# A weight sum queued behind an addition, and two norms' root products queued behind gate products, in the FFN inputs of a hybrid decoder layer

## The chip, the cores and the metric

The kernel runs on one core of a Trainium2 chip. The metric is device microseconds of one execution; three runs of the kernel before took 2287.8 to 2289.66 us, with a median of 2289.38 us. Lower is better. The engines are called as the profile calls them: PE is TensorE (PEld its weight loads), DVE is VectorE, ACT is ScalarE, POOL is GpSimd, and SP is SyncE, whose queue issues nearly all transfers.

## The reference

One layer for 1024 tokens of width 1024, all in float32: a SwiGLU half-step (ffn1), a mixer of three branches, and a second SwiGLU half-step (ffn2). Every part is normed before and after:

```python
def rms_norm(x, g):
    y = x * lax.rsqrt(jnp.mean(x * x, axis=-1, keepdims=True) + NORM_EPS)
    return y * g

def swiglu(u, w_in, w_out):
    gate, up = jnp.split(u @ w_in, 2, axis=-1)      # w_in: 1024 x 5632
    return (jax.nn.silu(gate) * up) @ w_out         # w_out: 2816 x 1024

f1 = swiglu(rms_norm(h, ffn1_pre_g), ffn1_w_in, ffn1_w_out)
h = h + 0.5 * rms_norm(f1, ffn1_post_g)
u = rms_norm(h, mix_pre_g)
# ... RWKV-7 time mixing, sliding-window attention and attention to memory,
#     all from u @ w_in, merged by gates and projected by w_out
h = h + rms_norm(merged @ w_out, mix_post_g)
f2 = swiglu(rms_norm(h, ffn2_pre_g), ffn2_w_in, ffn2_w_out)
h = h + 0.5 * rms_norm(f2, ffn2_post_g)
```

## The kernel before

**Products.** Activations lie with the features on the 128 partitions and the tokens on the free side, in two halves of 512 tokens (`TH`). A float32 product is made of three rounded ones: each operand is split into a high part (a cast on ACT, L277 for weights, L454 for activations) and a low part (a subtraction on DVE, L279 and L455), and `mm3` (L345) adds high x high, high x low and low x high into one PSUM bank (L348, L349, L350). A product of a weight operand (128 outputs, 4 blocks of 128 features) with a half of the activations is thus 4 x 3 = 12 matmuls.

**The seven products.** The FFN's products are done as 2 x 2 blocks with seven instead of eight block products. The activations' quarters are combined into factors (`b11`, `b21`, `t2`, `t1`, `t3`, `b22`, `t4`; made in `factors_first`, `factors_part` and `factors_end`, each then split), the weights' strips likewise. Only `b11` and `b21` need the first half of the tokens alone; all others need both halves, and so the second half's norm.

**The order of an FFN's input, `ffn_in` (L566).** First stand the norm of the second half (`norm`) and the factors. In ffn2 the norm is two: the mixer's post-norm and residual addition (`post_norm`), then the pre-norm (`factors_norm`). Then come the first two products of the gate for the first `FIRST` feature blocks j (9 in ffn1, 13 in ffn2), two products for each j, one with `b11` and one with `b21`: 18 and 26 products, 216 and 312 matmuls, which need no second half. Their results (`first`, L586) are copied out of PSUM by ACT and stored in DRAM (L587). After them come 22 steps (`ffn_in_pair`, L655). A step whose gate is already begun (kind "rest") makes five products in this order: t2 into px, t1 into pz, t3 onto px, b22 onto pz, t4 onto px. DVE copies px out with an addition after t2 (u, L673), pz after t1 (m, called z in the code), and adds px and z after t3:

```python
self.product(px, self.take(name, j), fs["t3"])
up = pool.tile([P, TH], F32, tag="up", name="up", bufs=2)
with self.tc.high_priority(offset=self.lead):
    V.tensor_tensor(up, px, z, ALU.add)                       # L686
self.product(pz, self.take(name, j), fs["b22"], last=True)
```

Then it adds pz (L689), multiplies by `up` (L691) and finishes the other half after t4. t4 writes onto px, so it waits for L686. The other steps (kind "pair") make their gate products themselves.

**The weights.** `operands` (L282) is a generator that loads raw strips (`raw`, five buffers, `w_raw`, loads on SP's queue, L268) and splits them; `take` lets it run eight operands ahead of the product (`OPS` = 8, buffers `w_hi`, `w_lo`). A step of kind "rest" needs four raw tiles a1, a2, b1, b2 and makes five operands of them: the first is the weight sum s = b1 + b2 (L303), then b1 = a1 - b1 (L304), a1 = s - a1 (L305), and a2 = a2 - a1 (L309). Since the generator runs eight operands ahead and a step uses five, the sum of step j + 2 is written in step j, just after `up`.

**The norms.** `inverse_root` (L426) takes the sum of squares, splits it (sq_hi on ACT, L438; sq_lo on DVE, L439), takes the mean over the partitions with two matmuls against a constant (the root products, L441), and forms the root with a logarithm, an exponential and a square on ACT (L444 to L446) and two DVE operations (L447, L448). It is used by all norms but the first over the memory and the last.

**What sets the order.** The program is written in one order; a planner then issues each engine's instructions in order of priority among those that are ready by its own reckoning of times, and puts in the semaphores. The priority is the place in the written order; `high_priority` moves what is written in it forward by some places (`lead` 300 for weights and parts of the chain, `urgent` 1000). `issue_after` keeps what it encloses behind a given instruction on that instruction's engine; `keep_in_program_order` keeps an instruction behind the one written before it on its engine. On the chip each engine works off its queue in the planned order and waits where an input is late.

Of the kernel before, what the change touches and what calls it, by code (L numbers as in the profile page):

```python
# [10 lines left out]
F32 = mybir.dt.float32  # L11
F32R = mybir.dt.float32r
I32 = mybir.dt.int32
ALU = mybir.AluOpType
# [15 lines left out]
SUMS = ("s1", "s2", "s3", "s4")  # L30
LAST_FORM = len(OUT_FORMS) - 1
FIRST = {"ffn1": 9, "ffn2": 13}
MIX_FIRST = (12, 13, 8, 4)
FILL = (18, 19, 14, 15)
HALVES = ((0, 0, TH), (1, 0, TH))
# [177 lines left out]
class Builder:  # L213
# [68 lines left out]
    def operands(self):  # L282
        V = self.nc.vector
        odd = False
        for name, i in self.seq:
            kind = name.partition("_")[2]
            odd = not odd and kind == "gate"
            a1 = self.raw(RAWS - 1 - (kind == "gate" and not odd))
            if kind == "out":
                kept = name == "ffn2_out" and i[0] == LAST_FORM and i[1] < KEEP  # L290
                yield (name, i), self.operand(a1, self.keep if kept else None)
                continue
            if kind == "gate":
                yield (name, i), self.operand(a1)
                continue
            a2 = self.raw(RAWS - 2)
            if kind != "rest":
                yield (name, i), self.operand(a1)
                yield (name, i), self.operand(a2)
            if kind in ("rest", "pair"):  # L300
                b1, b2 = self.raw(RAWS - 3), self.raw(RAWS - 4)
                s = self.sums.tile([P, 4, P], F32, tag="w_sum", name="w_sum", bufs=1)
                V.tensor_tensor(s, b1, b2, ALU.add)  # L303
                V.tensor_tensor(b1, a1, b1, ALU.subtract)  # L304
                V.tensor_tensor(a1, s, a1, ALU.subtract)  # L305
                yield (name, i), self.operand(a1)
                yield (name, i), self.operand(s)
                yield (name, i), self.operand(b1)
                V.tensor_tensor(a2, a2, a1, ALU.subtract)  # L309
                yield (name, i), self.operand(a2)  # L310
                yield (name, i), self.operand(b2)

    def prefetch(self, n=OPS, lead=None):
        with self.tc.high_priority(offset=self.lead if lead is None else lead):
# [30 lines left out]
    def mm3(self, out, w, x, first, last, **kw):  # L345
        (wh, wl), (xh, xl) = w, x
        mm = self.nc.tensor.matmul
        mm(out, wh, xh, start=first, stop=False, **kw)  # L348
        mm(out, wh, xl, start=False, stop=False, **kw)  # L349
        mm(out, wl, xh, start=False, stop=last, **kw)  # L350

    def project(self, w, u, outs, within={}):

# [72 lines left out]
    def inverse_root(self, sq, pool, between=None):  # L426
# [7 lines left out]
        with self.tc.high_priority(offset=self.lead):  # L434
            if not self.log_table:
                keep(S.preload_act_table_set("natural_log_exp_and_others"))
                self.log_table = True
            keep(S.activation(hi, sq, ACT.Identity, bias=self.eps))  # L438
            V.scalar_tensor_tensor(lo, sq, self.eps, hi.bitcast(F32), ALU.add, ALU.subtract)  # L439
            for i, x in enumerate((hi, lo)):  # L440
                mm = nc.tensor.matmul(ps, self.mean_r, x, start=i == 0, stop=i == 1)  # L441
                if between:
                    keep(mm)
            keep(S.activation(y, ps, ACT.Ln))  # L444
            keep(S.activation(y, y, ACT.Exp, scale=-0.5))
            keep(S.activation(sq, y, ACT.Square))  # L446
            V.scalar_tensor_tensor(sq, ps, -0.5, sq, ALU.mult, ALU.mult)  # L447
            V.scalar_tensor_tensor(y, sq, 1.5, y, ALU.add, ALU.mult)  # L448
# [117 lines left out]
    def ffn_in(self, f, x, form_d, first_d, parts, norm):  # L566

        nc, V = self.nc, self.nc.vector
        with self.tc.tile_pool(reuse_waits="tile", name="ffn_in", bufs=2) as pool:
            self.sums = pool  # L570
            self.factors_begin(pool)
            fs = self.fs
            for part in parts:
                norm(part, pool)
                self.factors_part(x, part, pool)
            self.factors_end(x)

            sums = {}
            for j, part in self.gate_order(FIRST[f]):
                if not part:  # L580
                    sums[j] = self.psum("px")
                self.product(sums[j], self.take(f + "_gate", (j, part)), fs["b21" if part else "b11"], not part, part > 0)
                tag, bufs = ("gate", 6) if part else ("px", 3)
                t = pool.tile([P, TH], F32, tag=tag, name="first", bufs=bufs)
                with self.tc.high_priority(offset=self.urgent):
                    nc.scalar.copy(t, sums[j])  # L586
                nc.sync.dma_start(first_d[j, part], t)  # L587
            self.log_table = False
            pairs = []
            for j in range(KF):  # L590
                *pair, made = self.ffn_in_pair(f, j, pool, first_d)
# [2 lines left out]
                    self.sums_made(f, j - FIRST[f], self.sums_loads(f, j - FIRST[f], pool, 4), made)  # L594
                if j % 2:
                    self.out_forms(j // 2, *pairs[-2:], pool, form_d)

    def sums_loads(self, f, q, pool, bufs):

# [55 lines left out]
    def ffn_in_pair(self, f, j, pool, first_d):  # L655
# [27 lines left out]
        self.product(px, self.take(name, j), fs["t3"])  # L683
        up = pool.tile([P, TH], F32, tag="up", name="up", bufs=2)
        with self.tc.high_priority(offset=self.lead):
            V.tensor_tensor(up, px, z, ALU.add)  # L686
        self.product(pz, self.take(name, j), fs["b22"], last=True)
        g1 = pool.tile([P, TH], F32, tag="gate", name="g", bufs=6)
        V.tensor_tensor(g1, pz, x, ALU.add)  # L689
# [954 lines left out]
    def build(self):  # L1644
        nc, tc, io = self.nc, self.tc, self.io
        with contextlib.ExitStack() as outer, tc.tile_pool(reuse_waits="tile", name="consts", bufs=1) as cp, \
# [2 lines left out]
            self.sum_d = {f: tc.dram_tile([len(SUMS), KP, P, KH, P], F32, name=f + "_sum_d") for f in ("ffn1", "ffn2")}  # L1649
            self.plan()  # L1650
            self.log_table, self.units, self.between = False, None, None
            self.vecs = cp.tile([P, NVEC], F32, name="vecs")
            nc.scalar.dma_start(self.vecs, io["vecs"])
            self.ones = cp.tile([P, 1], F32, name="ones")
# [138 lines left out]
```

## Time and profile before

| | |
|---|---|
| median of three runs | 2289.38 us (2287.8 to 2289.66) |
| the profiled execution's own time | 2288.03 us |
| its span, first to last instruction | 2286.3 us |
| mean granted clock of PE | 0.996 |
| PE busy | 2248.4 us, 98% |
| DVE, ACT busy | 1650.4 us, 996.6 us |
| transfers | 417.66 MB, 183 GB/s |

The profile is of one execution. In a list of waits, the columns are the waiting engine and its line, what ended the wait, the total in us, the number of waits, and the longest. In a timeline, they are the start in us from the span's start, the duration, engine, line, operation, output and inputs with their shapes and the count, and in brackets the idle time before it with what ended it. In a table of stretches, they are the stretch, its length, and the busy time with the number of instructions of PE, PEld, DVE, ACT and POOL, then the granted clock, the transfers' share and GB/s; a table for one tile on one engine has that engine alone. The tile z of the code appears as `m`, `x` as `u` or `px`, `up` as `up`. The gate products are the matmuls of px before the first step: from 40.2 us in ffn1 and from 1636.0 us in ffn2.

### The profile page before, as it was taken

What the parts mean: (1) busy time and instruction counts of PE and PEld (TensorE: products, weight loads), DVE (VectorE), ACT (ScalarE), POOL (GpSimd) and SP (SyncE); (2) the same over time, 40 slices, a digit from 0 to 9 for tenths busy, and PEclk for the clock granted to TensorE, in tenths of its full rate; (3) what the DMA queues carried; (4) which work ended last, traced back from release to release, by engine and by line L of the source; (5) the groups of instructions that cost most, each with busy time, mean ns of one, the idle gap of its engine ahead of it and who ended that gap; (6) DMA issues with size and microseconds to landing.
All of it is one profiled execution on the core that took longest, in us unless ns stands there. A gap on an engine that the chain in (4) does not pass through costs nothing.

```text
span 2286.3 us, 33447 instructions
## 1 busy us (share of the span) xinstructions
PE 2248.4 (98%) x11868; PEld 1842.3 (81%) x11868; DVE 1650.4 (72%) x2692; ACT 996.6 (44%) x1875; POOL 92.4 (4%) x138
## 2 busy tenths in 40 slices
PE   8999999999999999999999999999999999999998
PEld 6878888888888778888878877788788788888887
DVE  6987767666698885995665577675898885656676
ACT  5523333454555653223444454325663233345452
POOL 0000000000000000001320000041000000000000
PEclk9999999999999999999999999999999999999999
DMA  8565566686654466325436678755465552348663
GB/s 280 163 202 166 199 218 208 217 277 204 190 169 152 116 148 185 109 95 193 149 116 189 201 236 288 248 172 162 160 213 184 185 175 92 116 153 249 212 196 121
DMA packets 280775, 417.66 MB, mean 183 GB/s; under 512 B 82304, under 2 KB 104320, under 8 KB 280352
## 3 DMA queue, kind: packets, MB, share of 16 engines
q1 hardware_dynamic: 272832, 400.26, 55.2%
q10 hardware_dynamic: 7776, 15.28, 2.0%
q8 instruction: 93, 1.52, 0.3%
q14 instruction: 74, 0.61, 0.1%
HBM read 284.89 MB, written 129.50 MB: 181 GB/s over the span
## 4 chain that ended last, share of the span: by engine, by line
PE 77%; DVE 11%; DMA 7%; ACT 2%; issue 2%; SPq 0%; POOL 0%; DVEq 0%; ACTq 0%
PE px L348 6%; PE px L350 6%; PE px L349 6%; PE po L349 6%; PE po L348 6%; PE po L350 6%; PE pgate L348 3%; PE pgate L350 3%; PE pgate L349 3%; PE pz L348 2%; PE pz L350 2%; PE pz L349 2%; DMA w_raw<-in_ffn_in 2%; DVE w_lo L279 2%; PE pq L350 1%
## 5 line engine op out<-in xcount | busy, mean ns | idle before, releaser
L277 ACT CAST w_hi<-w_raw 128x512 fp32r<-128x512 f32 x594 | 366.8, 619 | 690.1 <-PE px L349 156.5
L279 DVE TENSOR_TENSOR w_lo<-w_raw,w_hi 128x512 fp32r<-128x512 f32 x594 | 411.7, 695 | 205.2 <-ACT w_hi L277 181.1
L350 PE MATMUL po<-u,w_lo 128*128 128x512 f32 (+1 forms) x476 | 180.9, 380 | 0.0
L349 PE MATMUL po<-u,w_hi 128*128 128x512 f32 (+1 forms) x476 | 180.9, 380 | 0.0
L348 PE MATMUL po<-u,w_hi 128*128 128x512 f32 (+1 forms) x476 | 180.9, 380 | 0.0
L348 PE MATMUL pgate<-u,w_hi 128*128 128x512 f32 x384 | 154.8, 403 | 0.0
L350 PE MATMUL pgate<-u,w_lo 128*128 128x512 f32 x384 | 151.5, 395 | 0.0
L349 PE MATMUL pgate<-u,w_hi 128*128 128x512 f32 x384 | 149.8, 390 | 0.0
L348 PE MATMUL px<-f,w_hi 128*128 128x512 f32 x352 | 138.0, 392 | 3.6 <-DVE up L686 2.7
L348 PE MATMUL px<-u,w_hi 128*128 128x512 f32 x352 | 137.0, 389 | 0.8 <-DVE km L1380 0.8
L348 PE MATMUL pz<-u,w_hi 128*128 128x512 f32 x352 | 137.0, 389 | 0.5 <-DVE m L673 0.5
L349 PE MATMUL px<-f,w_hi 128*128 128x512 f32 x352 | 137.2, 390 | 0.2 <-DVE f L455 0.2
L350 PE MATMUL px<-f,w_lo 128*128 128x512 f32 x352 | 137.0, 389 | 0.0
L350 PE MATMUL px<-u,w_lo 128*128 128x512 f32 x352 | 137.0, 389 | 0.0
L350 PE MATMUL pz<-u,w_lo 128*128 128x512 f32 x352 | 136.9, 389 | 0.0
L349 PE MATMUL px<-u,w_hi 128*128 128x512 f32 x352 | 136.9, 389 | 0.0
L349 PE MATMUL pz<-u,w_hi 128*128 128x512 f32 x352 | 136.9, 389 | 0.0
L455 DVE TENSOR_TENSOR u<-hid,u 128x512 fp32r<-128x512 f32 x114 | 78.3, 691 | 48.2 <-ACT u L454 47.5
L349 PEld LDWEIGHTS po<-u,w_hi 128*128 128x128 f32 x476 | 89.5, 188 | 17.2
L348 PEld LDWEIGHTS po<-u,w_hi 128*128 128x128 f32 x476 | 89.5, 188 | 17.1
L350 PEld LDWEIGHTS po<-u,w_lo 128*128 128x128 f32 x476 | 89.5, 188 | 16.8
L454 ACT CAST u<-hid 128x512 fp32r<-128x512 f32 x114 | 70.7, 620 | 66.2 <-DMA hid<-form_d 57.2
(391 smaller groups left out, 5125.8 us busy)
## 6 DMA issues: line engine op xcount, KB each, us to landing
w_raw<-in_ffn_in SPq DMA_DIRECT2D x220, 256.0 KB
hid<-form_d SPq DMA_DIRECT2D x154, 256.0 KB
w_raw<-in_win SPq DMA_DIRECT2D x112, 256.0 KB
form_d<-g SPq DMA_DIRECT2D x88, 256.0 KB
ws<-in_ffn_out SPq DMA_DIRECT2D x88, 256.0 KB
ffn_sum_d<-ws SPq DMA_DIRECT2D x88, 256.0 KB
w_raw<-ffn_sum_d SPq DMA_DIRECT2D x88, 256.0 KB
form_d<-h SPq DMA_DIRECT2D x66, 256.0 KB
```

Of the source, the lines that this page charges most:

```text
L277: self.nc.scalar.copy(hi, x)
L279: self.split_last = self.nc.vector.tensor_tensor(lo, x, hi.bitcast(F32), ALU.subtract)
L348: mm(out, wh, xh, start=first, stop=False, **kw)
L349: mm(out, wh, xl, start=False, stop=False, **kw)
L350: mm(out, wl, xh, start=False, stop=last, **kw)
L454: self.nc.scalar.copy(hi, x)
L455: self.nc.vector.tensor_tensor(lo, x, hi.bitcast(F32), ALU.subtract)
```

## The change

Two things change.

First, for steps of kind "rest" the weight sum L303 is written inside an `issue_after` on the latest `up` addition, so that on DVE it stands behind it (`behind_up`). Where no `up` has been written yet in this FFN, nothing is asked.

Second, the gate products become a generator (`gates_begin`) that gives back the last matmul of each `mm3`. The two root products of a norm are written inside an `issue_after` on one of these: the matmul that `PINS` names by its count, 78 for ffn1's norm, 42 and 114 for ffn2's two. `pinned` first writes as many gate products as that takes; so these, with their weights' loads, casts and splits and their copies and stores, now stand in the written order between the norm's split and its root products, ahead of the rest of the norm. What is left of the gate products follows the factors as before. The block of high priority in `inverse_root` is cut in two for this, in all norms.

```diff
+PINS = {"ffn1": (78,), "ffn2": (42, 114)}
...
                 s = self.sums.tile([P, 4, P], F32, tag="w_sum", name="w_sum", bufs=1)
-                V.tensor_tensor(s, b1, b2, ALU.add)
+                with self.behind_up(kind):
+                    V.tensor_tensor(s, b1, b2, ALU.add)
                 V.tensor_tensor(b1, a1, b1, ALU.subtract)
...
+    def behind_up(self, kind):
+
+        return self.tc.issue_after(self.up.ins) if kind == "rest" and self.up else contextlib.nullcontext()
...
-        mm(out, wl, xh, start=False, stop=last, **kw)
+        return mm(out, wl, xh, start=False, stop=last, **kw)
...
             V.scalar_tensor_tensor(lo, sq, self.eps, hi.bitcast(F32), ALU.add, ALU.subtract)
-            for i, x in enumerate((hi, lo)):
-                mm = nc.tensor.matmul(ps, self.mean_r, x, start=i == 0, stop=i == 1)
-                if between:
-                    keep(mm)
+        pinned = self.pinned()
+        with self.tc.high_priority(offset=self.lead):
+            with pinned:
+                for i, x in enumerate((hi, lo)):
+                    mm = nc.tensor.matmul(ps, self.mean_r, x, start=i == 0, stop=i == 1)
+                    if between:
+                        keep(mm)
             keep(S.activation(y, ps, ACT.Ln))
...
             self.factors_begin(pool)
-            fs = self.fs
+            self.gates_first, self.pins, self.gone = self.gates_begin(f, pool, first_d), list(PINS[f]), 0
             for part in parts:
                 norm(part, pool)
                 self.factors_part(x, part, pool)
             self.factors_end(x)
 
-            sums = {}
-            for j, part in self.gate_order(FIRST[f]):
...
-            self.log_table = False
+            for _ in self.gates_first:
+                pass
+            self.log_table, self.up = False, None
...
+    def gates_begin(self, f, pool, first_d):
+
+        nc, fs, sums = self.nc, self.fs, {}
+        for j, part in self.gate_order(FIRST[f]):
+            if not part:
+                sums[j] = self.psum("px")
+            w, x = self.take(f + "_gate", (j, part)), fs["b21" if part else "b11"]
+            for k in range(KH):
+                yield self.mm3(sums[j], tuple(t[:, k] for t in w), x[k], not part and k == 0, part > 0 and k == KH - 1, skip_group_check=True)
+            tag, bufs = ("gate", 6) if part else ("px", 3)
+            t = pool.tile([P, TH], F32, tag=tag, name="first", bufs=bufs)
+            with self.tc.high_priority(offset=self.urgent):
+                nc.scalar.copy(t, sums[j])
+            nc.sync.dma_start(first_d[j, part], t)
+
+    def pinned(self):
+
+        if not self.pins:
+            return contextlib.nullcontext()
+        n = self.pins.pop(0)
+        while self.gone < n:
+            behind, self.gone = next(self.gates_first), self.gone + 3
+        return self.tc.issue_after(behind.ins)
...
-            V.tensor_tensor(up, px, z, ALU.add)
+            self.up = V.tensor_tensor(up, px, z, ALU.add)
```

More of the change, by code (lines that the diff above doesn't have):

```diff
@@ L576, in ffn_in @@
             self.factors_end(x)
-            sums = {}
-            for j, part in self.gate_order(FIRST[f]):
[L580 to L587, printed above, removed]
-            self.log_table = False
+            for _ in self.gates_first:
+                pass
+            self.log_table, self.up = False, None
             pairs = []
@@ L1651, in build @@
             self.log_table, self.units, self.between = False, None, None
+            self.pins, self.up = [], None
             self.vecs = cp.tile([P, NVEC], F32, name="vecs")
```

## The prediction

> **What bounds the kernel now.** I read the page first, then what TensorE (PE) waited for, then VectorE's (DVE) waits, and then the timeline at the places which those name.
>
> ```profile
> span 2286.3 us, 33447 instructions
> PE 2248.4 (98%) x11868; PEld 1842.3 (81%) x11868; DVE 1650.4 (72%) x2692; ACT 996.6 (44%) x1875; POOL 92.4 (4%) x138
> PE 77%; DVE 11%; DMA 7%; ACT 2%; issue 2%; SPq 0%; POOL 0%; DVEq 0%; ACTq 0%
> ```
>
> PE is busy in 98% of the span and carries most of the chain. The change adds and removes no arithmetic, so all it can win are holes in PE's stream: 2286.3 - 2248.4 = 37.9 us at the very most. The waits of PE say which holes it can reach (columns: us in total, times, longest).
>
> ```profile
> PE ps_rs L441 <- ACT sq_hi L438: 3.9, 6, 1.5
> PE px L348 <- DVE up L686: 2.7, 5, 0.7
> PE px L348 <- ACT w_hi L277: 0.7, 2, 0.4
> PE pz L348 <- DVE m L673: 0.5, 1, 0.5
> PE px L349 <- DVE f L455: 0.2, 1, 0.2
> ```
>
> The first row is the root products that stand in PE's queue before their operand is there; the second and third are the last product of a step (t4), which adds onto px and so must wait until `up` has read it. The last two are waits on the norms' factors and on z, and will matter below.
>
> **Part 1: the sum behind `up`.** VectorE's own waits show what is in front of `up`:
>
> ```profile
> DVE w_sum L303 <- DMA w_raw<-in_ffn_in: 35.2, 27, 2.6
> ```
>
> The first weight sum waits for loads 27 times. One such place, VectorE first and then PE:
>
> ```profile
> 153.76 0.68 DVE L279 TENSOR_TENSOR w_lo<-w_raw,w_hi 128x512 fp32r<-128x512 f32 x1
> 157.03 0.69 DVE L303 TENSOR_TENSOR w_sum<-w_raw 128x512 f32<-128x512 f32 x1 [2.58 <-DMA w_raw<-in_ffn_in]
> 157.75 0.69 DVE L304 TENSOR_TENSOR w_raw<-w_raw 128x512 f32<-128x512 f32 x1
> 158.36 0.68 DVE L686 TENSOR_TENSOR up<-px,m 128x512 f32<-128x512 f32 x1
> 158.96 0.68 DVE L305 TENSOR_TENSOR w_raw<-w_sum,w_raw 128x512 f32<-128x512 f32 x1
> 161.01 0.68 DVE L689 TENSOR_TENSOR g<-pz,u 128x512 f32<-128x512 f32 x1
> ```
>
> ```profile
> 155.41 0.39 PE L350 MATMUL px<-f,w_lo 128*128 128x512 f32 x1
> 158.13 0.39 PE L350 MATMUL pz<-u,w_lo 128*128 128x512 f32 x1
> 159.19 0.47 PE L348 MATMUL px<-f,w_hi 128*128 128x512 f32 x1 [0.67 <-DVE up L686]
> ```
>
> px is complete at 155.41 + 0.39 = 155.8, `up` could run then, but VectorE sits at the sum until the load lands at 157.0, does the sum and L304, and reaches `up` at 158.36. PE has 12 matmuls of pz to hide behind (155.41 to 158.13, 2.72 us, so 0.227 each) and then stops: 1.06 us between starts instead of 0.23. The loss is 0.83 us, more than the 0.67 printed, since a matmul is recorded as 0.39 long but the next starts after 0.23. So each wait of this kind costs its idle time plus 0.16.
>
> With the sum behind `up`, `up` runs at 155.8 and ends before 156.6, 1.8 us before PE needs it: this hole closes. The two rows of px waits hold seven such holes, 2.7 + 0.7 = 3.4 us of idle, 3.4 + 7 x 0.16 = 4.5 us lost. (I count the two put down to w_hi here: the waits for `up` are the ones at the head of t4, and weights are fetched eight products ahead.) Holes too short to show as idle come on top, such as this pair, 0.52 apart, 0.29 lost:
>
> ```profile
> 1748.10 0.39 PE L350 MATMUL pz<-u,w_lo 128*128 128x512 f32 x1
> 1748.62 0.47 PE L348 MATMUL px<-f,w_hi 128*128 128x512 f32 x1
> ```
>
> That makes **-4.8 us**. [...]
>
> What is queued behind the sum, and now behind `up` as well: L304, L305, L309, the splits of the step's operands. The sum goes back by one VectorE addition at most where the load is late (0.69 us by its row), and by more only where the load was there first. It serves the step after the next; `up` of step j stands ahead of the sum of step j + 2. Seven products of 2.72 us, 19 us, lie between this sum and the first product that reads it, so I cost the delay at nothing; without that cover the 7 + 11 sums concerned would cost 18 x 0.69 = 12 us. The later releases of the raw buffers delay later loads by as much, under the same cover. What is late next is the following step's u and z, behind whatever VectorE still owes; through the steps it is not full,
>
> ```profile
> 106.90:200.00 93.10, 91.27 (x398) 74.11 (x398) 76.85 (x124) 29.62 (x50) 0.00 (x0) 1.00 0.58 191
> ```
>
> 76.85 of 93.10 us (the third pair), so it works off what gathers behind a late load, two or three additions, within a step. Bounds of the part: 0 and -5.3 (two more short holes of about 0.25).
>
> **Part 2: the pins.** In ffn1, PE, then ScalarE (ACT), then VectorE:
>
> ```profile
> 55.48 0.39 PE L349 MATMUL px<-u,w_hi 128*128 128x512 f32 x1
> 57.37 0.50 PE L441 MATMUL ps_rs<-sq_hi,mean_r 128*128 128x512 f32 x1 [1.50 <-ACT sq_hi L438]
> ```
>
> ```profile
> 56.59 0.72 ACT L438 ACTIVATE sq_hi<-sq,eps 128x512 fp32r<-128x512 f32 x1 [0.44 <-DVE sq L468]
> 58.75 0.60 ACT L444 ACTIVATE rs<-ps_rs 128x512 f32<-128x512 f32 x1 [1.43 <-PE ps_rs L441]
> 60.24 0.62 ACT L277 CAST w_hi<-w_raw 128x512 fp32r<-128x512 f32 x1
> 60.75 0.64 ACT L446 ACTIVATE sq<-rs 128x512 f32<-128x512 f32 x1
> ```
>
> ```profile
> 60.89 0.69 DVE L279 TENSOR_TENSOR w_lo<-w_raw,w_hi 128x512 fp32r<-128x512 f32 x1 [2.79 <-ACT w_hi L277]
> ```
>
> The hole is 57.37 - 55.48 - 0.23 = 1.66 us. In ffn2 there are two:
>
> ```profile
> 1643.71 0.39 PE L349 MATMUL px<-r,w_hi 128*128 128x512 f32 x1
> 1644.76 0.50 PE L441 MATMUL ps_rs<-sq_hi,mean_r 128*128 128x512 f32 x1 [0.66 <-ACT sq_hi L438]
> ...
> 1668.93 0.39 PE L349 MATMUL px<-u,w_hi 128*128 128x512 f32 x1
> 1669.81 0.50 PE L441 MATMUL ps_rs<-sq_hi,mean_r 128*128 128x512 f32 x1 [0.49 <-ACT sq_hi L438]
> ```
>
> 0.82 and 0.65 us. How many gate matmuls stand ahead of each root product (stretches of px alone, count in brackets):
>
> ```profile
> 40.10:55.70 15.60, 15.51 (x68) 1.00 0.72 228
> 1636.00:1643.90 7.90, 7.89 (x35) 1.00 0.43 138
> 1644.90:1669.20 24.30, 24.03 (x105) 1.00 0.79 262
> ```
>
> Now 68, 35 and 35 + 105 = 140; the pins ask for 78, 42 and 114. Ten more in ffn1 are 2.27 us: the product starts near 55.48 + 11 x 0.227 = 57.98, after its operand (57.31). Seven more in ffn2: 1645.5 against 1644.8 now. Neither delays the second half of the root by more than 0.1. The third pin, 114, is already met by 140 and binds nothing; that hole closes only if the planner keeps its distance of 105 from the first root, now seven later. So up to 1.66 + 0.82 + 0.65 = 3.13 us of holes go.
>
> But what comes next is late too. After the roots VectorE has the factors to make and hardly a gap:
>
> ```profile
> 61.50:94.30 32.80, 32.80 (x146) 27.18 (x145) 32.71 (x55) 18.68 (x34) 0.00 (x0) 1.00 0.58 178
> 1674.00:1709.40 35.40, 35.40 (x158) 29.32 (x157) 35.27 (x59) 23.10 (x43) 0.00 (x0) 1.00 0.57 177
> ```
>
> The third pair of figures is VectorE's: 32.71 of 32.80 and 35.27 of 35.40 us. PE reaches the first products on those factors sooner, and where VectorE has not moved it waits there (the f and m rows above). In ffn1 VectorE does move: tracing the gates first puts the cast of 60.24 ahead of the logarithm, into ScalarE's 1.43 us idle, so the square of 60.75 comes about 0.5 earlier and the split of 60.89 falls into VectorE's 2.79 us of idle: about 0.5 + 0.6 = 1.1. I keep 1.0 of 1.66 (ends: 0 and 1.66). In ffn2 no such shift shows; I keep 0.6 of 1.47 (ends 0 and 1.47). Part 1 helps ffn1 once more: the sum stands between two factors,
>
> ```profile
> 98.98 0.68 DVE L455 TENSOR_TENSOR f<-t,f 128x512 fp32r<-128x512 f32 x1
> 99.69 0.69 DVE L303 TENSOR_TENSOR w_sum<-w_raw 128x512 f32<-128x512 f32 x1
> 100.31 0.68 DVE L455 TENSOR_TENSOR f<-t,f 128x512 fp32r<-128x512 f32 x1
> ```
>
> and steps out of their way (0.6 us of VectorE); I count it as part of the 1.0.
>
> Gate work now traced ahead of the rest of the norm: its loads and the copies' stores pass the residual's stores on SP's queue, its casts and copies the norm's operations on ScalarE, its splits those on VectorE. Casts and splits wait for operand buffers that PE frees one per product, so few can pass; I take 0, bounds -0.6 to +1.2 (one split earlier, two splits ahead of the factors). POOL gets nothing. The other norms have no pin; their root products only move by a few places in priority, taken as 0.
>
> **Sum.** -4.8 - 1.0 - 0.6 = -6.4 us against the profiled execution's 2288.03 (span 2286.3): 2281.6. The median of the runs lies 1.35 above it, so **2283.0**.
>
> **The rivals.**
> *The wait is handed on.* `up` is free, but VectorE still stands at the sum until the load lands, and L689, L691 and the next step's u and m queue behind it; PE stops there instead. [...] Against: L689 has until its px and pz buffers come round, and that z waits only once (0.5) today. It leaves the pins' 1.6: 2287.8.
> *The pins give everything back.* PE only arrives sooner at factors that are as late as before. For: the full stretches. Against: the idle 2.79. Part 1 alone: 2289.38 - 4.8 = 2284.6.
> *The change does not do what it says.* The planner had put the roots where the inputs are ready by its reckoning and moves other work with them; nothing is left: 2289.
> *Slower: the gate splits crowd the norm.* Traced first, they pass the factors on a VectorE that is full from 61.5 to 94.3. Each takes 0.6 (98.98 to 99.69 is one place); PE waits for the last factor. It decides from 6.4 / 0.6 = 11 splits that pass; at 20 the kernel is 5.6 us slower, 2295. Against: the buffers let one pass per product.
>
> **Chances and range.** Forecast 0.54, its own range 2280.8 to 2284.7; handed on 0.13; given back 0.14; nothing 0.08; slower 0.11. About 0.2%, 4.6 us, is what a measurement of this kernel can tell: faster means below 2284.8. That is the forecast and most of the given-back case: 0.64; within: 0.26; slower (0.11, less the cases of it that cost little): 0.10. The low end takes every hole: 4.8 + 0.5 + 3.13 + 0.6 = 9.0, so 2280.3; the high end reaches to the cases with no gain, 2289.5.
>
> **What would show it.** Right: no px wait for `up` in the waits of PE; `up` directly ahead of L303 in VectorE's order in steps with loads, and still about 35 us of waits for w_raw; the roots behind 78, 42 and about 147 gate matmuls with no idle ahead; px and pz waits for f and m grown by 1 to 2 us. Wrong: waits of PE for w_lo or u in the steps, factors later by more than PE gained, or a different order in the mixer.

## The result

The changed kernel takes 2280.31 us (median; 2272.83 to 2281.52) where the kernel before takes 2289.38 us beside it: a ratio of 0.9956, 95% interval 0.9944 to 0.9968. It is faster by 0.44%, some 10 us by the ratio and 9.07 by the two medians; the forecast was 2283.0, 6.4 us less than before. The direction was right, and so was which holes close; how much of them is kept was not: the median lies at the end of the range that stood for "every hole goes" (2280.3), and by the ratio (0.9956 x 2289.38 = 2279.3) the time lies 1 us below it.

The profiled execution took 2280.59 us. Its page, in the lines that answer to those shown of before:

```profile
span 2278.6 us, 33469 instructions
PE 2244.7 (99%) x11868; PEld 1843.1 (81%) x11868; DVE 1648.2 (72%) x2692; ACT 994.9 (44%) x1875; POOL 92.1 (4%) x138
PE 86%; DVE 7%; DMA 4%; ACT 2%; issue 2%; SPq 0%; POOL 0%; DVEq 0%; ACTq 0%
```

The instructions are the same 11868 matmuls and 2692 of VectorE. PE's share of the chain went from 77 to 86%, VectorE's from 11 to 7. What PE waited for (us in total, times, longest), and below it the wait of VectorE for the weights of the sum:

```profile
PE ps_rs L450 <- ACT sq_hi L444: 1.5, 4, 0.6
...
PE px L355 <- DVE f L464: 0.8, 1, 0.8
...
PE px L354 <- DVE up L711: 0.6, 1, 0.6
```

```profile
DVE w_sum L305 <- DMA w_raw<-in_ffn_in: 9.4, 14, 1.3
```

VectorE's wait for PE ahead of `up`, before and after:

```profile
DVE up L686 <- PE px L350: 38.0, 24, 1.7
```

```profile
DVE up L711 <- PE px L356: 52.5, 36, 1.7
```

The lines have moved: the sum L303 is now L305, `up` L686 is L711, the root product L441 is L450, sq_hi L438 is L444, u and m L673 are L698, the splits' L455 is L464. Of the px waits for `up` one of 0.6 us is left, in the last pair of ffn1 (457.90 us), outside the steps of kind "rest"; no root product of the FFN inputs waits any more (the four that are left are in other norms). The second fence holds what the prediction did not foresee: it expected about 35 us of waits for w_raw to stay, and 9.4 are left. The idle time has in part moved: VectorE waits 52.5 us ahead of `up` where it waited 38.0. The place that corresponds to the one the prediction showed, VectorE and then PE:

```profile
150.90 0.68 DVE L280 TENSOR_TENSOR w_lo<-w_raw,w_hi 128x512 fp32r<-128x512 f32 x1
152.73 0.69 DVE L711 TENSOR_TENSOR up<-px,m 128x512 f32<-128x512 f32 x1 [1.14 <-PE px L356]
153.51 0.69 DVE L305 TENSOR_TENSOR w_sum<-w_raw 128x512 f32<-128x512 f32 x1
```

```profile
155.02 0.39 PE L356 MATMUL pz<-u,w_lo 128*128 128x512 f32 x1
155.25 0.39 PE L354 MATMUL px<-f,w_hi 128*128 128x512 f32 x1
```

VectorE now idles for PE's product and no longer for the load, `up` starts as soon as px is complete, and by the time `up` is done the load is there, so the sum waits for next to nothing. PE goes from pz to t4 in 0.23 us. The three roots:

```profile
56.73 0.39 PE L356 MATMUL px<-r,w_lo 128*128 128x512 f32 x1
56.95 0.39 PE L450 MATMUL ps_rs<-sq_hi,mean_r 128*128 128x512 f32 x1
...
1642.81 0.39 PE L356 MATMUL px<-u,w_lo 128*128 128x512 f32 x1
1643.04 0.39 PE L450 MATMUL ps_rs<-sq_hi,mean_r 128*128 128x512 f32 x1
...
1668.20 0.39 PE L355 MATMUL px<-r,w_hi 128*128 128x512 f32 x1
1668.42 0.44 PE L450 MATMUL ps_rs<-sq_hi,mean_r 128*128 128x512 f32 x1
```

They stand behind 78, 42 and 152 gate matmuls, 0.22 to 0.23 us after the matmul before them. All three holes are shut.

Where the time went, stage by stage, in us from the start of a stage's first matmul to that of the next stage's. "Before 2" and "after 2" are later profiles of the same two kernels; the other columns are experiments told below. The last row is no part of the change: the mixer between the two FFNs.

| stage | before | before 2 | after | after 2 | sum alone | pins alone | no edge | ffn2's pins |
|---|---|---|---|---|---|---|---|---|
| ffn1 gates | 51.42 | 50.20 | 49.50 | 49.58 | 50.48 | 49.53 | 50.39 | 50.65 |
| ffn1 steps 0, 1 | 27.86 | 28.34 | 28.48 | 29.02 | 27.76 | 28.75 | 27.93 | 27.59 |
| ffn1 steps 2 to 8 | 98.30 | 97.15 | 95.20 | 95.20 | 95.20 | 98.19 | 95.20 | 95.20 |
| ffn2 gates | 73.48 | 73.46 | 71.79 | 71.85 | 73.48 | 71.86 | 73.48 | 71.86 |
| ffn2 step 0 | 14.36 | 14.18 | 13.79 | 13.94 | 14.19 | 14.42 | 13.60 | 13.78 |
| ffn2 steps 1 to 12 | 166.36 | 166.25 | 163.21 | 163.22 | 163.20 | 166.96 | 163.20 | 163.21 |
| sum of these | 431.78 | 429.58 | 421.97 | 422.81 | 424.31 | 429.71 | 423.80 | 422.29 |
| mixer | 869.23 | 868.68 | 871.11 | 867.84 | 866.54 | 868.62 | 868.04 | 863.25 |

The mean of the two profiles of before is 430.68, of the two of after 422.39: 8.3 us, 0.36%, which both measured intervals of this kernel (here and in the second group below) hold. The mixer differs by up to 8 us between runs, so a single pair of spans would not do. 95.20 and 163.2 us are floors at the steady pace of these steps, in which no 12 matmuls in a row, start to start, took less than 2.71 us in the first profiles of before and after: steps 2 to 8 are 7 x 60 = 420 matmuls and steps 1 to 12 are 720, and at 0.2267 us each (12 in 2.72 us, as in the prediction) these take 95.2 and 163.2.

### The profile page after: what moved, and what is told of

It is laid out like the page before. It is cut to its first block, busy times and chain, and to the rows that moved or that the text cites. A ratio compares the mean times of both kernels' runs of the same rounds, so it can differ in the third digit from the quotient of the medians.

```text
span 2278.6 us, 33469 instructions
## 1 busy us (share of the span) xinstructions
PE 2244.7 (99%) x11868; PEld 1843.1 (81%) x11868; DVE 1648.2 (72%) x2692; ACT 994.9 (44%) x1875; POOL 92.1 (4%) x138
## 4 chain that ended last, share of the span: by engine, by line
PE 86%; DVE 7%; DMA 4%; ACT 2%; issue 2%; SPq 0%; POOL 0%; DVEq 0%; ACTq 0%
PE px L354 7%; PE px L355 7%; PE px L356 7%; PE po L355 6%; PE po L354 6%; PE po L356 6%; PE pz L356 3%; PE pz L354 3%; PE pz L355 3%; PE pgate L354 3%; PE pgate L356 3%; PE pgate L355 3%; PE pq L355 1%; PE pq L356 1%; PE pq L354 1%
## 5 line engine op out<-in xcount | busy, mean ns | idle before, releaser
L464 DVE TENSOR_TENSOR u<-hid,u 128x512 fp32r<-128x512 f32 x114 | 78.3, 690 | 47.1 <-ACT u L463 46.1
```

Source lines behind the costliest of these rows:

```text
L464: self.nc.vector.tensor_tensor(lo, x, hi.bitcast(F32), ALU.subtract)
```

## The experiments

**The parts.** Four kernels ran on one chip with the kernel before, 2286.46 us there. The sum alone:

```diff
-PINS = {"ffn1": (78,), "ffn2": (42, 114)}
+PINS = {"ffn1": (), "ffn2": ()}
```

> Part 1 alone: the sums stand behind up, no root product is pinned and the gate products are written where they were. If the holes at t4 simply close (my present theory): the steps of kind rest get shorter by about 3.1 us in ffn1 and 3.1 us in ffn2, as in the changed kernel, the gate stretches keep their three holes (1.66, 0.82, 0.65), and the whole is 6.2 us faster. If the prediction's term was right: 4.8 us. If the wait is handed on: the steps keep their length, with PE waiting for m, u or w_lo, and the whole is within 1 us of before.

2277.83 us, ratio 0.9965 (0.9951 to 0.9978). Both stretches of steps are at their floors, 95.20 and 163.20; the gates keep their holes. So part 1 is worth 3.10 + 3.16 = 6.26 us against the first profile of before, and 1.95 + 3.05 = 5.0 us against the second, whose holes in ffn1 were fewer. The pins alone:

```diff
-        return self.tc.issue_after(self.up.ins) if kind == "rest" and self.up else contextlib.nullcontext()
+        return self.tc.issue_after(self.up.ins) if False else contextlib.nullcontext()
```

> Part 2 alone: the roots are pinned at 78, 42 and 114, the sums stay ahead of up. Present theory: the gate stretch gets 1.9 us shorter in ffn1 and 1.7 in ffn2; the first step gives 0.6 back in ffn1 and nothing in ffn2, the t4 holes stay, and the whole is 3 to 3.5 us faster. The prediction's term: 1.6 us, with 0.7 given back in ffn1 and 0.9 in ffn2. If the pins give everything back: 0.

2282.60 us, ratio 0.9985 (0.9975 to 0.9996). The steps stay at least as long as before (98.19 and 166.96); the gates lose what they lose in the changed kernel. The two parts act on different stages, and by the ratios they add: 0.35 + 0.15 = 0.50% against 0.44 (0.32 to 0.56). By the stretches, against the mean of the two profiles of before, the sum alone wins 6.4 us, the pins alone 1.0 and both 8.3: in the one profile of the pins alone, the steps lose 1.9 of the 2.9 us that the gates win.

**The edge without its effect on PE.** The gate products are written as early as in the changed kernel, but the root products are bound to none:

```diff
-        return self.tc.issue_after(behind.ins)
+        return contextlib.nullcontext()
```

> The changed kernel without the edges that hold the root products back; the gate products are still written ahead of them. If the edge is what closes the holes: the roots stand behind 68, 35 and 140 gate matmuls again, with holes of 1.66, 0.82 and 0.65 us, and the whole is like part 1 alone, about 6.2 us faster than before. If the written order is what brings it: no holes, about 9 us faster.

2278.35 us, ratio 0.9975 (0.9963 to 0.9986). The roots stand behind 68, 35 and 140 gate matmuls again, as before, and the gate stretches are 50.39 and 73.48. So the edge, not the place in the written order, moves the roots and shuts the holes. Step 0 of ffn2, however, has 13.60 us here and 13.78 to 13.94 with pins in ffn2, against 14.19 with the sum alone, one profile each: the wait for z there (0.5 us in the waits of before) goes because the gate products are written earlier, and needs no pin. (With the pins alone, step 0 has 14.42 us: the wait for z is gone there too, but PE waits for a factor instead: 0.9 us in two waits for f in that profile, 0.2 in one in before.)

**Later pins.**

```diff
-PINS = {"ffn1": (78,), "ffn2": (42, 114)}
+PINS = {"ffn1": (102,), "ffn2": (66, 114)}
```

> The changed kernel with the first root of each FFN pinned 24 gate matmuls later (102 and 66), 24 x 0.227 = 5.4 us. If the full VectorE behind the roots is the bound, as the prediction had it: what PE does behind the gate products is 5.4 us later in both FFNs, in all 10.9 us slower than the changed kernel. If the factors are finished well before their products in ffn2 (they were by 8 us in the kernel before): 3 to 5 us slower in ffn1 and under 1 us in ffn2.

2286.96 us, ratio 0.9999 (0.9985 to 1.0013): the gain is gone. But not where it was expected: the gate stretches are 49.54 and 71.80 us, as in the changed kernel, and the first steps cost 1 us more in ffn2 and nothing in ffn1 (14.75 and 28.47). The loss lies steps later, 99.26 us for steps 2 to 8 and 171.17 for 1 to 12. PE, VectorE and SP's queue at the largest place:

```profile
1748.45 0.39 PE L356 MATMUL pz<-u,w_lo 128*128 128x512 f32 x1
1753.72 0.80 PE L354 MATMUL px<-f,w_hi 128*128 128x512 f32 x1 [4.88 <-DVE u L698]
```

```profile
1745.96 0.69 DVE L662 TENSOR_TENSOR h<-g,h 128x512 f32<-128x512 f32 x1
1752.97 0.69 DVE L698 TENSOR_TENSOR u<-px,m 128x512 f32<-128x512 f32 x1 [6.32 <-DMA m<-first_d]
```

```profile
1746.68 0.32 SPq L664 DMA_DIRECT2D form_d<-h  x1
1747.05 0.45 SPq L664 DMA_DIRECT2D form_d<-g  x1
1747.55 1.24 SPq L689 DMA_DIRECT2D m<-first_d  x2
```

PE waits for u, u for the stored gate product m, and the reload of m was issued at 1747.55 only, behind stores (L664) of what VectorE had just finished at 1746.65. The edit has changed the order of SP's queue too: with these pins the third reload of m in ffn2 stands behind seven of those stores, in the changed kernel behind one.

**The changed kernel again, and four small changes of it,** on a second chip, where the kernel before took 2286.98 us. First the kernel itself:

> The changed kernel once more, on the chip on which the others of this group run, so that they are compared with it and not only with the kernel before. Theory A (the gain is a property of the two edits): 0.9955 to 0.9965 of the kernel before, with step stretches of 95.2 us in ffn1 and 163.2 us in ffn2 (98.3 and 166.4 before). Theory B (a good part of the measured gain was a faster clock in some runs): 0.998, with the same stretches but a longer mixer. Theory C (the pins are worth nothing beside the sum): the same 0.9965 as the sum alone had, to 0.0005.

2276.86 us, ratio 0.9962 (0.9947 to 0.9977), with the stretches of the table. Theory A holds; the mixer was 867.84, not longer than in before, so theory B has no support. Theory C can't be told from A by the times; by the stretches the pins bring 424.31 - 422.39 = 1.9 us.

The third pin left out:

```diff
-PINS = {"ffn1": (78,), "ffn2": (42, 114)}
+PINS = {"ffn1": (78,), "ffn2": (42,)}
```

> The third pin left out, so ffn2's second root product is bound to no gate product. The prediction's theory (the third pin is met anyway and binds nothing): the second root still stands behind 152 gate matmuls with no idle time ahead, ffn2's gate stretch stays at 71.8 us, and the time is that of the changed kernel within 0.5 us. Rival (the pin's tracing of gate work ahead of the second norm is what keeps the distance): the 0.65 us hole comes back, 72.4 us, and step 0 of ffn2 goes from 13.8 to 14.4 us.

2280.53 us, ratio 0.9969 (0.9957 to 0.9982); ffn2's gates take 71.84 us, step 0 14.05. The stretch between the two roots (its length, and PE's busy time with the count of px) is

```profile
1637.55:1662.60 25.05, 24.87 (x110) 1.00 0.84 280
```

110 matmuls, with the 42 before them 152, as with the pin. It binds nothing.

The sum behind `up` in steps of both kinds:

```diff
-        return self.tc.issue_after(self.up.ins) if kind == "rest" and self.up else contextlib.nullcontext()
+        return self.tc.issue_after(self.up.ins) if self.up else contextlib.nullcontext()
```

> The sum stands behind the addition of px and z in steps of both kinds. In the planned order this moves it in one place of each FFN. The wait-goes theory: the one wait for the addition that is left in the changed kernel, 0.96 us between starts near 457 us of ffn1, goes as the seven others did: 0.7 us less in the stretch of ffn1's pairs, nothing in ffn2, 2279.5 where the changed kernel has 2280.3. The handed-on theory: the next sums and splits are late, and PE waits for w_lo in the pair behind, 0 to +0.5 us.

2279.81 us, ratio 0.9972 (0.9963 to 0.9982). No wait for `up` is left, but none is in the second profile of the changed kernel either, and VectorE's work ahead of that `up` is a split (L464 at 456.56 us, after 1.17 us of idle for ScalarE), not a sum. So this run shows nothing of the edit; the expectation had taken a wait of one execution for a property of the kernel. It does show something of ffn1's pin: ScalarE waited 2.36 us for the store ahead of the squares (0.88 and 1.57 in the two profiles of the changed kernel), the root product, behind 78 gate matmuls as there, came 0.38 us after the matmul before it, and its second half waited again (0.79 us between starts). The gates took 50.36 us, as without the pin. So 78 shuts ffn1's hole only while that store is not later than it was in the other runs.

Four more VectorE instructions in the factors of each FFN (the output is unchanged, but the planner also moves other work), 2.4 us by an estimate of 0.6 each, the distance of three 128x512 subtractions on VectorE in the changed kernel (starts at 118.14, 118.74 and 119.34 us):

```diff
-            V.tensor_tensor(self.t2[k], x21[k], self.t2[k], ALU.subtract)
+            V.tensor_tensor(self.t2[k], x21[k], self.t2[k], ALU.subtract); V.tensor_tensor(self.t2[k], self.t2[k], self.t2[k], ALU.max)
```

> Four more VectorE instructions (the maximum of a tile with itself, 128x512, 0.6 us each) in the factors of each FFN: 2.4 us more for VectorE behind the roots, the output unchanged. Theory full engine (the prediction's: VectorE is full behind the roots, so PE must wait for whatever is later there): steps 0 and 1 of ffn1 go from 28.5 to 30.9 us and step 0 of ffn2 from 13.8 to 16.2 us, 4.8 us in all. Theory due times (VectorE works ahead of PE in ffn2; the last factor of t4 starts at 1717.8 us, 1.8 us before PE needs it): ffn1, where PE already waits 1.2 us for a factor, pays 1.8 to 2.4 us, and ffn2 pays 0 to 0.6 us.

2286.43 us, ratio 0.9993 (0.9981 to 1.0005). In ffn2, step 0 takes 14.27 us (13.78 to 14.05 in the kernels with the sum's edge and these pins) and steps 1 to 12 163.22: at most 0.5 of the 2.4 us, so a full VectorE is not what PE waits for there. In ffn1 steps 0 and 1 take 28.11, no more than in the changed kernel, and there both theories fail: the price, 7.05 us, is paid in steps 2 to 8 (102.25 us), by one hole. PE, VectorE, SP's queue, and PE's clock behind the hole (stretch, length, busy times with counts, granted clock):

```profile
127.34 0.39 PE L356 MATMUL pz<-u,w_lo 128*128 128x512 f32 x1
132.24 0.79 PE L354 MATMUL px<-f,w_hi 128*128 128x512 f32 x1 [4.51 <-DVE u L698]
```

```profile
125.94 0.69 DVE L662 TENSOR_TENSOR h<-g,h 128x512 f32<-128x512 f32 x1
131.49 0.69 DVE L698 TENSOR_TENSOR u<-px,m 128x512 f32<-128x512 f32 x1 [4.87 <-DMA m<-first_d]
```

```profile
124.72 2.25 SPq L664 DMA_DIRECT2D form_d<-h  x3
127.02 0.45 SPq L664 DMA_DIRECT2D form_d<-g  x1
127.52 1.25 SPq L689 DMA_DIRECT2D m<-first_d  x2
```

```profile
132.30:137.00 4.70, 4.70 (x11) 3.73 (x12) 1.08 (x2) 0.00 (x0) 0.00 (x0) 0.50 0.12 45
```

It is the picture of the late pins: 4.90 - 0.23 = 4.67 us of hole, and then 11 matmuls in 4.70 us where 4.70 / 0.2267 = 20.7 would run, another 9.7 x 0.2267 = 2.2 us.

The two pictures share one more thing, which the times alone hide. In the changed kernel the third reload of ffn1 went out ten microseconds sooner, behind a single store:

```profile
117.05 0.33 SPq L664 DMA_DIRECT2D form_d<-g  x1
117.42 0.43 SPq L689 DMA_DIRECT2D m<-first_d  x1
```

In the busier kernel it stands behind all seven stores of that pair of steps, the last of them at 127.02. The planner had put it there, so four added instructions changed the order of SP's queue and not only the times. In every kernel with its reloads on SP's queue that has no such hole, before and the changed kernel among them, the third reload of each FFN stands behind one store; with the late pins it stands behind two in ffn1 (a hole of 2.50 - 0.23 = 2.27 us) and behind seven in ffn2 (5.04 us). The busier kernel's ffn2, where the same four instructions cost 0.5 us at most, kept the old order.

**The reload on another queue,** to see whether SP's order makes the price. On a third chip, before at 2285.97 us there; in the busier kernel and in the one with the late pins:

```diff
-            nc.sync.dma_start(m1, first_d[j, 0])
-            nc.sync.dma_start(g0, first_d[j, 1])
+            nc.gpsimd.dma_start(m1, first_d[j, 0])
+            nc.gpsimd.dma_start(g0, first_d[j, 1])
```

> The busier kernel (four more VectorE instructions in the factors), with the reloads of the stored gate products (the tile m and its gate) issued from GpSimd's queue and not from SP's. In the busier kernel steps 2 to 8 of ffn1 took 102.25 us where the changed kernel has 95.20, with one wait of TensorE of 4.5 us for u; u waited for a reload that SP issued at 127.52 us, behind stores of products which VectorE finished at 126.6; the buffer of the reload was free from 124.1. Theory queue (2.4 us of VectorE became 7 because the reload stood behind those stores): the reload goes out 3.4 us earlier, the wait falls from 4.5 to about 1 us, the stretch to 96 to 98 us, the time to 2281 to 2283 on a chip where the busier one has 2286.4. Theory backlog (VectorE owes the work, the queue is nothing): the stretch stays at 101 to 103 us and the time at 2286.

2294.37 us, ratio 1.0042 (1.0027 to 1.0058).

> The kernel with the late pins (102 and 66), with the same reloads on GpSimd's queue. With the late pins steps 2 to 8 of ffn1 took 99.26 and steps 1 to 12 of ffn2 171.17 us (95.20 and 163.21 in the changed kernel). Theory queue (the late pins cost little by themselves; the cost is the reload behind the stores): most of 4.1 + 8.0 us goes, the stretches fall to 95.2 to 97 and 163.2 to 167 us, the time from 2287 to 2279 to 2282. Theory backlog: they stay within 1 us of what they were.

2298.18 us, ratio 1.0056 (1.0035 to 1.0078). Both are slower, against the queue theory; the backlog theory has one stretch right and neither time. In the busier kernel the hole itself shrank, from 4.67 to 1.58 us: the reload was issued at 121.52, as soon as its buffer was free, and not at 127.52, and landed 4.5 us later. (The 124.1 of the expectation is when the buffer of the next reload came free.) What PE waits for is still u:

```profile
124.98 0.39 PE L356 MATMUL pz<-u,w_lo 128*128 128x512 f32 x1
126.79 0.50 PE L354 MATMUL px<-f,w_hi 128*128 128x512 f32 x1 [1.42 <-DVE u L698]
```

but steps 2 to 8 took 102.21 us all the same and ffn2's steps 173.08 (163.22 without the move), by new waits. VectorE's wait for the sum's weights, in the kernel with the reloads moved and then in the busier kernel:

```profile
DVE w_sum L305 <- DMA w_raw<-in_ffn_in: 39.4, 24, 5.3
```

```profile
DVE w_sum L305 <- DMA w_raw<-in_ffn_in: 7.4, 15, 1.0
```

With the late pins the hole of 5.04 us in ffn2 became one of 3.26 - 0.23 = 3.03, that in ffn1 grew from 2.27 to 2.60 us, and the stretches 100.37 and 177.66. So the reload's place in SP's queue is a part of the hole's length in two of three places, but its price could not be taken away by this edit, since SP's order changed with it and weights came late instead. What makes those loads late was not tried, nor was a kernel in which the third reload alone is put back behind the first store, so what the planner's order costs by itself stays open.

**Ffn2's pins alone beside the sum.**

```diff
-PINS = {"ffn1": (78,), "ffn2": (42, 114)}
+PINS = {"ffn1": (), "ffn2": (42, 114)}
```

> The changed kernel with ffn1's pin left out and ffn2's kept. Theory given back in ffn1 only (TensorE comes 0.9 us sooner to ffn1's steps and waits 0.6 to 1.1 us more for a factor there; in ffn2 the whole 1.7 us is kept): gate stretches of 50.4 us in ffn1 and 71.8 us in ffn2, steps 0 and 1 of ffn1 back to 27.9 us from 28.5 to 29.0, so the time is that of the changed kernel to 0.5 us. Rival (ffn1's pin is worth its hole, 0.7 to 1.7 us): steps 0 and 1 stay at 28.5 and the kernel is 1 to 1.5 us slower than the changed one.

2273.27 us, ratio 0.9953 (0.9935 to 0.9972). Steps 0 and 1 of ffn1 are back to 27.59 us while its gates have 50.65. Ffn1's gates and first two steps together take 78.24, 78.32 and 78.24 us without its pin (sum alone, no edge, this one) and 77.98, 78.60 and 78.15 with it (after, after 2, third pin left out; 78.91 in the run above in which the store came 2.36 us late): the same. The pin of ffn1 is given back in full, and this version cannot be told from the changed kernel; in its profiled execution, 2270.97 us, what is shorter is the mixer, 863.25 us, which the edit does not touch.

**The kernel before again.**

> The kernel before once more, for a second profile of it. The reading to be tested: ffn1's hole at the root product (1.66 us in the first profile, but 0.73 and 0.65 us in the kernels without ffn1's pin) is not of one size; it follows a store that ScalarE waits for (1.59 us idle ahead of the squares in the first profile, 0.66 us in the kernel with the sum alone). If so, the hole here lies between 0.6 and 1.7 us, and the idle of ScalarE ahead of the squares moves with it. If it is 1.66 us again, the split of the block of high priority shortened it. The holes in the steps (98.3 and 166.4 us) and the two of ffn2's roots (73.5 us) should stand to 0.2 us in either case.

ScalarE's wait ahead of the squares, and PE at ffn1's root:

```profile
45.88 2.72 ACT L464 ACTIVATE sq<-acc 128x512 f32<-128x512 f32 x5 [0.37 <-DMA vm_d<-vm]
```

```profile
53.69 0.39 PE L349 MATMUL px<-u,w_hi 128*128 128x512 f32 x1
54.36 0.51 PE L441 MATMUL ps_rs<-sq_hi,mean_r 128*128 128x512 f32 x1 [0.28 <-ACT sq_hi L438]
```

The hole is 54.36 - 53.69 - 0.23 = 0.44 us, not 1.66. It is ScalarE's idle and 0.07 more in five profiles without ffn1's pin: 0.37 and 0.44 here, 0.58 and 0.65 (no edge), 0.66 and 0.73 (sum alone), 0.81 and 0.87 (ffn2's pins), 1.59 and 1.66 (the first profile of before). ffn1's hole follows the lateness of a store, which differs from one execution to the next. ffn2's holes stood, as expected: 1.04 - 0.23 = 0.81 and 0.87 - 0.23 = 0.64. The steps of ffn2 stood too (166.25), those of ffn1 did not (97.15 against 98.30).

## Why the prediction was right or wrong

By the stretches the change is worth 8.3 us where the sum forecast 6.4. Three steps of the sum failed, and each is answered below: ffn2's pins, of which too little was kept (0.6 against 1.65), the size of part 1 (4.8 against 5.6), and ffn2's step 0, put at nothing (0.4). Ffn1's pins failed the other way (1.0 against 0.6 or nothing).

**Part 1, -4.8 us: the mechanism right, the term too small.** It measured 6.26 us in the profile that the prediction used. The step that failed is the count of "seven such holes" with 0.16 us each and one short one. Ten cost over 0.1 us, five in ffn1 (0.16, 0.46, 0.83, 0.56, 0.62) and five in ffn2 (0.29, 0.85, 0.80, 0.15, 0.37), 5.1 us by their starts. And each costs a little more than the gap ahead of it: in all ten, the start after that comes 0.30 or 0.31 us later and not 0.23. Of before, right behind the first row that the prediction showed of this hole:

```profile
159.50 0.40 PE L349 MATMUL px<-f,w_hi 128*128 128x512 f32 x1
```

159.50 - 159.19 = 0.31 us, 0.08 above the usual 0.23. Ten times 0.08 is 0.8, and 5.1 + 0.8 = 5.9 of the 6.26; the rest is in gaps below 0.1. Counting the stretch against its floor (98.30 - 95.2 and 166.36 - 163.2) would have given 6.26 at once, from rows that were there. The second profile has 5.0, so about 1 us of the term is the run's.

**The sum's delay, "I cost the delay at nothing",** held: the steps stand at their floors, so neither the sum nor the releases behind it were late for PE.

**Pins in ffn2, "no such shift shows; I keep 0.6 of 1.47": this step failed.** All of it was kept, 73.48 to 71.79, 1.69 us with the slower matmuls behind the holes. The argument was that VectorE is busy in 35.27 of 35.40 us and so PE, coming sooner, must wait. VectorE is that full, but with work that is not due: with 2.4 us more of it PE lost 0.5 us at most. Step 0 even became 0.4 us shorter (the means of the two profiles each), by the z wait that went with the early writing of the gates, which I had costed at nothing.

**Pins in ffn1, "I keep 1.0 of 1.66": wrong the other way.** The hole went, but PE waits for a factor instead. Of after:

```profile
94.58 0.39 PE L355 MATMUL px<-u,w_hi 128*128 128x512 f32 x1
95.79 0.50 PE L355 MATMUL px<-f,w_hi 128*128 128x512 f32 x1 [0.82 <-DVE f L464]
```

1.21 - 0.23 = 0.98 us lost, 1.53 in the second profile. The step that failed is "in ffn1 VectorE does move". The cast was to go ahead of the logarithm, but it stayed behind it, and the split still waited (ScalarE, then VectorE, of after):

```profile
57.67 0.60 ACT L453 ACTIVATE rs<-ps_rs 128x512 f32<-128x512 f32 x1 [0.99 <-PE ps_rs L450]
58.83 0.61 ACT L278 CAST w_hi<-w_raw 128x512 fp32r<-128x512 f32 x1
```

```profile
59.47 0.69 DVE L280 TENSOR_TENSOR w_lo<-w_raw,w_hi 128x512 fp32r<-128x512 f32 x1 [2.49 <-ACT w_hi L278]
```

VectorE's idle there is 2.49 us where it was 2.79. The norm's last operation (L448, now L457) ends 62.91 - 40.19 = 22.72 us after the first gate matmul in before and 61.90 - 39.19 = 22.71 us in after; the second profiles have 21.48 and 22.76. PE came sooner to factors that came no sooner, and later where the store had been in time without the pin. The rival "the pins give everything back" holds for this FFN and fails for the other. The two misses on the pins nearly cancel, which is luck: 1.6 forecast, 1.9 by the stretches of the sum alone and of after.

**The sum.** By terms, forecast and measured (the means of the two profiles of each kernel): part 1 4.8 and 5.6; ffn1's gates and first two steps 1.0 and 0.6 (0 against the kernels that lack only its pin); ffn2's pins 0.6 and 1.65; ffn2's step 0 nothing and 0.4. Together 6.4 and 8.3; what the medians show beyond that, 9.07, lies within the spread of the rest of the kernel.

**The rivals.** "Handed on": no wait of VectorE's moved to PE in the steps. "Does not do what it says": the edge moved the roots and the sum as written. "Slower: the gate splits crowd the norm": not at these pins. With pins 24 matmuls later the whole gain goes, so work written early does have a price; it was paid where no prediction looked, steps later, at a reload that the planner had put behind more stores on SP's queue.

**What was to show it.** Right: no wait for `up` in the steps of kind "rest", `up` directly ahead of the sum in them, the roots behind 78, 42 and about 147 (152). Wrong: the w_raw waits fell to 9.4 us, and the waits for f and m were to grow by 1 to 2 us. The f wait grew by 0.6 and 1.2 us in the two profiles, but the m wait of 0.5 (z) went, so the two together grew by 0.1 and 0.7.

## What to carry to other kernels

An engine that is busy all the time is not yet a bound (VectorE was busy here in 35.27 of 35.40 us, and 2.4 us more of work cost 0.5 at most): what counts is how long before its use each of its outputs is ready, and a few added instructions measure that. For a stretch with a steady pace, take its length against the count of matmuls at that pace; the sum of the printed waits leaves out short gaps (0.15 and 0.29 us here) and the late start behind each (0.08). And when work is written earlier, follow the transfers on the shared queue for several steps: a load stands behind what the planner has put ahead of it there (ffn1's third reload went out at 117.42 us behind one store in the changed kernel, and at 127.52 behind seven in the busier one), and a small edit elsewhere can change that order. Here the same 2.4 us of VectorE cost 7.05 us in the FFN where the third reload had moved behind seven stores, and 0.5 at most in the one where it had not.

## What the runs showed of the hardware

The granted clock was lower behind some holes of PE and not behind others. Behind the hole of 4.90 us above it was 0.50 for 4.7 us, in which 11 matmuls ran. A hole of 3.26 us between starts in the kernel with late pins and moved reloads, one of 3.81 in the busier one with moved reloads, and one of 2.50 (128.52 to 131.01) in the kernel with late pins were followed by these (stretch, length, busy times with counts, granted clock):

```profile
1740.83:1744.50 3.67, 3.67 (x10) 2.96 (x11) 2.94 (x5) 0.00 (x0) 0.54 (x1) 0.59 0.94 312
```

```profile
1878.80:1884.00 5.20, 5.17 (x16) 4.11 (x17) 4.47 (x8) 1.77 (x3) 0.00 (x0) 0.67 0.13 48
```

```profile
131.60:135.10 3.50, 3.50 (x10) 2.76 (x9) 0.00 (x0) 0.00 (x0) 0.00 (x0) 0.51 0.97 315
```

The granted clock was 0.59, 0.67 and 0.51. Behind two holes longer than the last it was 1.00: one of 2.83 us (127.84 to 130.67, late pins and moved reloads) and one of 3.16 (199.01 to 202.17, busier with moved reloads) were followed by these:

```profile
130.70:136.00 5.30, 5.30 (x23) 4.40 (x24) 5.00 (x9) 0.00 (x0) 0.55 (x1) 1.00 0.82 268
```

```profile
202.20:207.00 4.80, 4.80 (x21) 3.99 (x22) 4.70 (x8) 1.67 (x3) 0.00 (x0) 1.00 0.06 21
```

So between 2.5 and 3.2 us the length of a hole did not decide here whether the clock behind it was lower. What did, no run here shows.

The same order of work took different times: the changed kernel and the one with ffn2's pins alone have the same planned order on every engine in the mixer, and it took 871.11, 867.84 and 863.25 us. The waits for loads there differ: in the first of these, VectorE waited 3.36 us for a load of gin (L1530, at 1474.20 us), and PE then waited 1.15 and 2.04 us for gin; in the last, no two matmuls from 1455 to 1512 us start more than 0.37 us apart. One stretch of the mixer, in the first profile of the changed kernel and in the kernel with ffn2's pins alone:

```profile
1475.00:1490.00 15.00, 12.96 (x49) 10.22 (x50) 9.54 (x14) 1.36 (x3) 4.20 (x3) 0.89 0.73 231
```

```profile
1475.00:1490.00 15.00, 15.00 (x68) 12.43 (x67) 10.81 (x12) 1.87 (x3) 5.02 (x3) 1.00 0.53 172
```

Each stretch is cut at the same time of its own span, so the work in it is not quite the same; the first shows idle time and a granted clock of 0.89, the second neither. So a difference of up to 8 us between two executions with the same order in the mixer (871.11 against 863.25) says nothing of an edit elsewhere.
